# Hybrid mLSTM and pooling step: u, v and the gates begin with two contraction steps of one channel tile

## The chip, the cores and the metric

The kernel runs on one core of one Trainium2 chip. The metric is the device time of one execution, in microseconds (us); several runs of the same program are taken and their median is compared. TensorE multiplies matrices, VectorE and ScalarE work element by element, GpSimd does little here, and SyncE (SP) issues most of the transfers from the chip's main memory.

## What is computed

One step of a flow-matching backbone for 128 prompt tokens and 256 sample tokens, D = 2048 channels, in float32. Everything between the first norm and the output is one layer:

```python
mod = jax.nn.silu(cond) @ ada_w + ada_b          # shift, scale, gate for attention and MLP, 2048 each
h = _rmsnorm(x, norm_w[0]) * (1 + scale_a) + shift_a
proj = h @ w_in
q, k, v, o, g, u = jnp.split(proj, [M, 2 * M, 3 * M, 4 * M, 4 * M + N_GATES * N_HEADS], axis=-1)
...
mix = jnp.concatenate([hm, hp], axis=-1) @ w_out
x = x + gate_a * _rmsnorm(mix, norm_w[1])
h = _rmsnorm(x, norm_w[2]) * (1 + scale_f) + shift_f
y = jnp.square(jax.nn.relu(h @ w1)) @ w2
x = x + gate_f * _rmsnorm(y, norm_w[3])
```

hm comes from a bidirectional mLSTM over q, k, v and the gates g, hp from pooling u. The prompt and the sample have their own conditioning vectors, so every channel has two shifts and two scales.

## The kernel before, in words

**Precision.** Every large product is made of three: each operand is split into a high part (a copy to a narrower form, on ScalarE) and a low part (the difference, on VectorE), and hi·hi, hi·lo and lo·hi are added in PSUM (lines 379 to 381). `load_w` (line 114) loads a weight tile into one of three `raw` buffers from SP's queue (line 120) and splits it (lines 126 and 127).

**The adaLN product** `ada_mat` (line 203) multiplies the two conditioning vectors, as narrow stationary windows of 32 columns, with tiles of `ada_w`. Line 207 sets the tile: for `nk` channel tiles it is 128 partitions by 8/nk contraction rows by 128·nk channels, always 512 KB. A step of two channel tiles needs eight such tiles for shift and scale together, each with four products (eight instructions, line 218). They come from SP's queue (line 214) into four buffers with the tag "ada"; in the very first step half of them use the four buffers "lo". After the last tile ScalarE copies the sums (line 223), TensorE turns them into columns (line 226) and VectorE adds the bias and the norm's weight (lines 234 and 239). The function is a generator: each `next` emits one tile, the last two the copy and the columns. With nk = 2 that is nine `next`, with nk = 1, by line 207, five: four tiles of eight products each.

**x.** Three tiles of 128 tokens are loaded, their squares summed, and `transpose_x` (line 304) turns one channel tile with three TensorE transposes (line 307) and a copy out of PSUM, on ScalarE for odd tiles (line 310) and on VectorE for even ones (line 312). The string `X_ORDER` (line 32) says in which order transposes ("t"), adaLN steps ("a") and the broadcast of the norm factors ("b", lines 196 and 321) are issued. Up to `order.close()` (line 364), TensorE, VectorE and ScalarE run in exactly this order; behind it, and on SP's queue throughout, the builder's scheduler orders the instructions, by the order of the code and by when it takes them to be ready.

**h, u, v and gates.** `ksteps` (line 276) lists eight steps of two channel tiles. `make_h` (line 332) makes h of one step: hm (line 338) on VectorE, hh (line 343) on ScalarE, hl (line 344) on VectorE. In the first call the low part of u's first weights is computed between (line 341). The loop of line 367 runs over the steps, and in each over five chunks: two of u (512 columns each), then v with 384, 384 and 256 columns, the last with the 32 gate columns. A chunk loads its weights, multiplies them into three PSUM banks (one per token tile), and adds the banks into u and v in SBUF: copies on ScalarE in the first step (line 392), adds on VectorE in the others (line 394), gates in line 396. Behind the first three chunks stand three adaLN steps each for the next step's channels (`ADA_STEPS`, line 31), behind the fourth `make_h` of the next step (line 385). Eight PSUM banks serve everything.

The rest (q, k and attention with pooling and gates beside them, o, the output projection, the MLP) follows from line 398 on and isn't touched.

Of the kernel before, what the change touches and what calls it, by code (L numbers as in the profile page):

```python
# [15 lines left out]
KT = D // P  # L16
# [13 lines left out]
N_ADA = 4  # L30
ADA_STEPS = (3, 3, 3, 0, 0)
X_ORDER = "tatatatabtatatatat"
N_VEC = 4
# [5 lines left out]
def hymba_kernel(  # L39
# [20 lines left out]

    # ---------------------------------------------------------------- constants and small inputs
    cst = const.tile([P, N_CST, P], F32, name="cst")
# [32 lines left out]

    # silu(c); for every contraction tile in a row of zeros, so that a window of 32 columns puts it in any pair of rows
    cT = const.tile([P, 16, 38], F32, name="cT")
# [7 lines left out]

    # per-channel parameters as columns: prmT [128, 80 | 96]
    prmT = const.tile([P, 176], F32, name="prmT")
# [4 lines left out]

    # ---------------------------------------------------------------- helpers
    def load_w(pieces, name, n=1024, after=(), later=None):
        """pieces: (column offset in the tile view, dram AP [128, a, b]); returns the hi and lo parts."""
        raw = wp.tile([P, 1024], F32, tag="raw", name=f"raw_{name}", bufs=3)
# [25 lines left out]
    class Feed:  # L142
        """Side work, emitted in steps between the tiles of a large product."""

# [13 lines left out]
    def gemm_T(w, cols, xs, n, evac, feeds=(), korder=(0, 1, 2, 3), name="g", hold=None):  # L158
        """Transposed products: for every 256-column group, out[128 channels, n] in two tiles; groups share the k loop."""
        wv = wview(w)  # L160
# [24 lines left out]
    def rstd_cols(out, ss, n, scale):  # L185
        """out = (ss * scale + eps) ** -0.5, [128, n]"""
        nc.vector.tensor_scalar(out, ss, scale, EPS, op0=ALU.mult, op1=ALU.add)
        nc.gpsimd.tensor_tensor(out, out, mhalf[:, 0:n], op=ALU.pow)

    def bcast_row(col, name, ps=None):  # L190
        """PSUM tile with [p, 128 i + t] = col[t, i] for every partition p."""
        dg = slot(f"dg_{name}")
        dgv = dg[:, 0:NTOK].rearrange("p (i t) -> p i t", t=P)
        nc.vector.tensor_tensor(dgv, ident.unsqueeze(1).to_broadcast([P, 3, P]), col.unsqueeze(2).to_broadcast([P, 3, P]), op=ALU.mult)
        ps = bank(f"bc_{name}") if ps is None else ps
        nc.tensor.matmul(ps[:, 0:NTOK], ones, dg[:, 0:NTOK], start=True, stop=True)
        return ps

    # ---------------------------------------------------------------- adaLN
    mod = const.tile([P, 6, KT, 2], F32, name="mod")  # L200
    aw = ada_w.rearrange("(p j) n -> p j n", j=16)

    def ada_mat(parts, tags=("ada",)):
        """parts: up to four (i, first channel tile), nk channel tiles each, on the tensor engine.
        Row 32 g + 2 b + (0: ctx, 1: latent) of ps holds part b's sum over the contraction tiles j = g (mod 4)."""
        n, nk = len(parts), parts[0][2]
# [24 lines left out]
    def ada_finish(i, k0, nk, ps):  # L231
        """ps [128, nk, 2]: matrix product columns -> mod[i], with what the channel's norm weight adds to it"""
        v = mod[:, i, k0:k0 + nk, :]
# [10 lines left out]
    def ada_vec(i, q):  # L244
        """512 channels, on the vector engine; the tensor engine adds up the partitions"""
        acc = wp.tile([P, 2, 512], F32, tag="adaacc", name=f"ada_acc_{i}_{q}", bufs=1)
# [27 lines left out]

    # ---------------------------------------------------------------- x: statistics and transposes
    ksteps = [(k, 2) for k in range(0, KT, 2)]
    NS = len(ksteps)

    def first_ada():
# [42 lines left out]

    # ---------------------------------------------------------------- h, and u, v, gates (token-major), k outermost
    h = []
# [39 lines left out]
    order.close()  # L364
    for k in range(len(xT), KT):
        transpose_x(k)
    for s in range(NS):
        for ci, (kind, c0, w) in enumerate(chunks):
# [6 lines left out]
            for k in range(nk):  # L375
                xh, xl = h[k0 + k]
                for i in range(3):
# [3 lines left out]
                    nc.tensor.matmul(acc[i][:, 0:n], xl[:, sl], hi[:, k, :], start=False, stop=k == nk - 1)  # L381
            for _ in range(ADA_STEPS[ci]):
                next(ada0, None)
# [15 lines left out]

    # ---------------------------------------------------------------- pooling mixer  # L400
    mix = [None] * KT
# [22 lines left out]

    # ---------------------------------------------------------------- gate rows, stabilisers
    tokc = ((0, 1, 2), (0, 2, 1))
# [76 lines left out]

    # ---------------------------------------------------------------- q, k and attention
    q_sb, k_sb = [None] * NH, [None] * NH
# [15 lines left out]
    def attention(hp):  # L521
        """Two heads."""
        h0 = 2 * hp
# [44 lines left out]
        def update(i, d, wk):  # L568
            """state after the chunk at token tile i in direction d"""
            out = att.tile([P, 2, 129], F32, tag="C", name=f"C1_{hp}_{i}_{d}", bufs=5)  # L570
# [109 lines left out]

    # ---------------------------------------------------------------- o
    mixs = [None] * KT
# [25 lines left out]

    # ---------------------------------------------------------------- output projection
    for k in range(8):  # L710
# [33 lines left out]
    def token_rstd_rows(accs, name, between=None):  # L744
        """PSUM tile with (mean over channels + eps) ** -0.5 of every token, on all partitions"""
        ps = bank(f"tr_{name}")
# [14 lines left out]

    # ---------------------------------------------------------------- gate_f * norm_w[3] as rows
    mlp = ctx.enter_context(tc.tile_pool(name="mlp", bufs=2))
# [12 lines left out]

    # ---------------------------------------------------------------- residual and the MLP's input
    xr = []
# [56 lines left out]

    # ---------------------------------------------------------------- MLP
    hid = {}
# [98 lines left out]
    def done(i, a, b, side=iter(())):  # L936
        """square sum and gate of finished columns, a step of other work in between"""
        jk = mlp.tile([P, 512], F32, tag="jk", name=f"jky{i}_{a}", bufs=1)
        n = a // 512 + (a % 512 > 0)
        nc.scalar.activation(jk[:, 0:b - a], y[i][:, a:b], AF.Square, accum_out=ssy[:, i, n:n + 1])  # L940
        next(side, None)
        nc.vector.tensor_tensor(y[i][:, a:b], y[i][:, a:b], gf[min(i, 1), a // 1024][:, a % 1024:a % 1024 + b - a], op=ALU.mult)
# [6 lines left out]
    def residual(i):  # L949
        """norm and residual of a token tile, in pieces"""  # L950
        dst = y_prompt[0] if i == 0 else y_sample[0, (i - 1) * P:i * P]
# [5 lines left out]
    def last_part(ws):  # L957
        """the last 512 columns, token tile by token tile; the last tile in halves"""
        side = iter(())
# [88 lines left out]
```

## Time and profile before

| | |
|---|---|
| runs | 1767.98 us median of 3 (1766.83 to 1768.8) |
| profiled execution, first to last instruction | 1766.4 us, its own whole time isn't given apart from this span |
| mean granted TensorE clock | 0.994 |
| moved from main memory | 313.98 MB read, 184 GB/s over the span |
| start of the first step's u products | 30.71 us |
| steps of the loop of line 367 begin at | 30.71, 55.73, 78.53, 104.11 us ... |

The profile lists each instruction by its line, engine and operand names, "out<-in". PE is TensorE's matmul unit, DVE VectorE, ACT ScalarE, SPq the sync engine's queue. A row of the time view gives the start, the duration, the instruction and, in brackets, the idle time ahead of it and what ended it; instructions of one kind are merged ("x20"). A row of the view by stretches gives the length, then busy time and count of PE, weight loads, DVE, ACT and POOL, the granted clock, the busy share of the DMA engines and GB/s; asked for one line, only the engines that run it appear. In the view of waits a row names who waited for whom, the sum, the number of times and the longest. In the chain of waits that ended last, a row gives start, length and what the chain went through. Matmul durations include their latency: products that follow each other overlap, and their spacing is less than the duration.

### The profile page before, as it was taken

How to read it: one execution, taken by the hardware profiler on the slowest of the kernel's cores; microseconds unless marked ns; L12 is line 12 of the kernel's file. 1: busy time of each engine (PE TensorE's matmuls, PEld its weight loads, DVE VectorE, ACT ScalarE, POOL GpSimd, SP SyncE). 2: the span in 40 equal slices, each digit the busy share in tenths (PEclk: the TensorE clock that was granted, in tenths of full speed). 3: DMA queues.
4: the chain of work that ended last, by engine and by line, in shares of the span. 5: the costliest groups of instructions: out<-in, count | busy, mean ns of one | idle time of the engine just before them, and what ended most of it. 6: DMA issues, size and time to landing. Idle time of an engine off the chain costs nothing.

```text
span 1766.4 us, 24738 instructions
## 1 busy us (share of the span) xinstructions
PE 1719.2 (97%) x9643; PEld 1539.2 (87%) x9643; DVE 1067.4 (60%) x1756; ACT 627.3 (36%) x1047; POOL 129.7 (7%) x172
## 2 busy tenths in 40 slices
PE   6999999998999999999999999999999999999997
PEld 3777898887999989988988988988988998998986
DVE  3667877787898849763546644475444443443446
ACT  4322343443434336532432432332332332332332
POOL 0000021222101133110000000000000000000100
PEclk9999999999999999999999999999999999999999
DMA  9888988887777774574345544454434354344543
GB/s 304 279 263 286 299 261 231 253 251 213 232 238 235 237 250 156 185 225 131 120 130 162 175 130 121 130 167 122 129 120 131 120 168 131 120 130 136 165 141 107
DMA packets 250436, 326.15 MB, mean 185 GB/s; under 512 B 14096, under 2 KB 185808, under 8 KB 249936
## 3 DMA queue, kind: packets, MB, share of 16 engines
q1 hardware_dynamic: 242096, 303.74, 54.1%
q0 software_dynamic: 6560, 18.97, 4.3%
q10 hardware_dynamic: 1664, 1.87, 0.3%
q8 instruction: 75, 1.23, 0.3%
q14 instruction: 41, 0.34, 0.1%
HBM read 313.98 MB, written 10.55 MB: 184 GB/s over the span
## 4 chain that ended last, share of the span: by engine, by line
PE 86%; DMA 5%; issue 3%; DVE 2%; POOL 2%; ACT 1%; SPq 0%; ACTq 0%; DVEq 0%; POOLq 0%
PE y L855 10%; PE y L856 10%; PE y L857 10%; PE acc_w L135 9%; PE acc_w L137 9%; PE acc_w L136 9%; DMA ada_raw<-in_ada_w_dram 3%; PE acc_wo L135 3%; PE acc_wo L136 2%; PE acc_wo L137 2%; PE ada L218 2%; PE acc_o L135 1%; PE acc_o L137 1%; PE acc_o L136 1%; PE u L379 1%
## 5 line engine op out<-in xcount | busy, mean ns | idle before, releaser
L127 DVE TENSOR_TENSOR lo_w<-raw_w,hi_w 128x1024 fp32r<-128x1024 f32 x256 | 313.9, 1226 | 440.7 <-ACT hi_w L126 440.3
L126 ACT ACTIVATE hi_w<-raw_w 128x1024 fp32r<-128x1024 f32 x256 | 271.3, 1060 | 666.2 <-PE acc_w L136 302.1
L135 PE MATMUL acc_w<-h2h,hi_w 128*128 128x386 f32 x1024 | 347.8, 341 | 2.4 <-ACT h2h L805 2.4
L137 PE MATMUL acc_w<-h2h,lo_w 128*128 128x386 f32 x1024 | 347.5, 339 | 0.0
L136 PE MATMUL acc_w<-h2l,hi_w 128*128 128x386 f32 x1024 | 347.2, 339 | 0.0
L257 DVE SCALAR_TENSOR_TENSOR ada_acc<-ada_raw,sg,ada_acc 128x512 f32<-128x512 f32 x330 | 237.5, 767 | 21.8 <-DMA ada_raw<-in_ada_w_dram 21.7
L135 PEld LDWEIGHTS acc_w<-h2h,hi_w 128*128 128x128 f32 x1024 | 193.9, 190 | 5.2 <-ACT h2h L805 3.0
L136 PEld LDWEIGHTS acc_w<-h2l,hi_w 128*128 128x128 f32 x1024 | 193.8, 189 | 0.9 <-issue 0.4
L137 PEld LDWEIGHTS acc_w<-h2h,lo_w 128*128 128x128 f32 x1024 | 193.5, 189 | 0.0
L218 PE MATMUL ada<-ada_raw,cT 128*32 128x256 f32 x832 | 61.5, 397 | 5.1 <-DMA ada_raw<-in_ada_w_dram 5.0
L879 DVE TENSOR_TENSOR y<-y,y 128x512 f32<-128x512 f32 x81 | 55.7, 691 | 11.8 <-PE y L857 11.3
L126 ACT ACTIVATE hi_wo<-raw_wo 128x1024 fp32r<-128x1024 f32 x32 | 34.1, 1067 | 67.1 <-PE acc_wo L136 27.9
L846 ACT ACTIVATE z<-z,bz 128x128 f32<-128x128 f32 (+1 forms) x128 | 47.9, 442 | 11.3 <-DVE z L844 11.2
L127 DVE TENSOR_TENSOR lo_wo<-raw_wo,hi_wo 128x1024 fp32r<-128x1024 f32 x32 | 38.7, 1218 | 19.3 <-ACT hi_wo L126 19.3
L379 PE MATMUL v<-hi_v,hh 128*128 128x384 f32 (+1 forms) x144 | 49.0, 341 | 0.0
L381 PE MATMUL v<-hi_v,hl 128*128 128x384 f32 (+1 forms) x144 | 47.2, 328 | 0.0
L380 PE MATMUL v<-lo_v,hh 128*128 128x384 f32 (+1 forms) x144 | 46.9, 326 | 0.0
L774 POOL DMA_DIRECT2D gf_dram<-gfT x1 | 0.5, 519 | 626.8 <-DVE bz L843 626.8
L135 PE MATMUL acc_k<-hh,hi_k 128*128 128x384 f32 x128 | 45.4, 355 | 0.0
L218 PEld LDWEIGHTS ada<-ada_raw,cT 128*32 128x32 f32 x832 | 19.8, 110 | 28.9 <-issue 14.5
L135 PE MATMUL acc_o<-hh,hi_o 128*128 128x384 f32 x128 | 44.7, 349 | 0.0
L135 PE MATMUL acc_q<-hh,hi_q 128*128 128x384 f32 x128 | 44.4, 347 | 0.0
(940 smaller groups left out, 3621.1 us busy)
## 6 DMA issues: line engine op xcount, KB each, us to landing
raw_w<-in_w_dram SPq DMA_DIRECT2D x256, 512.0 KB, 3.7
ada_raw<-in_ada_w_dram SPq DMA_DIRECT2D x192, 512.0 KB, 5.1
raw_wo<-in_w_out_dram SPq DMA_DIRECT2D x32, 512.0 KB, 4.9
raw_u<-in_w_in_dram SPq DMA_DIRECT2D x16, 512.0 KB, 7.4
raw_q<-in_w_in_dram SPq DMA_DIRECT2D x16, 512.0 KB, 5.8
raw_k<-in_w_in_dram SPq DMA_DIRECT2D x16, 512.0 KB, 5.2
raw_o<-in_w_in_dram SPq DMA_DIRECT2D x16, 512.0 KB, 5.3
raw_v<-in_w_in_dram SPq DMA_DIRECT2D x16, 384.0 KB, 7.8
```

The costliest lines, as they stand in the source:

```text
L126: nc.scalar.activation(hi[:, 0:n], raw[:, 0:n], AF.Copy)
L127: low = lambda: nc.vector.tensor_tensor(lo[:, 0:n], raw[:, 0:n], hi[:, 0:n].bitcast(F32), op=ALU.subtract)
L135: nc.tensor.matmul(ps, lh, rh, start=start, stop=False)
L136: nc.tensor.matmul(ps, lh, rl, start=False, stop=False)
L137: mm3.ins = nc.tensor.matmul(ps, ll, rh, start=False, stop=stop).ins
L218: nc.tensor.matmul(ps[32 * g:32 * g + 32, 0:w], cT[:, j, 6 - 2 * b:38 - 2 * b], raw[:, a, :], start=b == 0 and j < 4, stop=b == n - 1 and ...
L257: nc.vector.scalar_tensor_tensor(acc[:, g, :], raw[:, a, :], cj, acc[:, g, :], op0=ALU.mult, op1=ALU.add)
L379: nc.tensor.matmul(acc[i][:, 0:n], xh[:, sl], hi[:, k, :], start=k == 0, stop=False)
L855: nc.tensor.matmul(acc, xh[:, s], hi, start=k == 8 * ch, stop=False)
L856: nc.tensor.matmul(acc, xh[:, s], lo, start=False, stop=False)
L857: nc.tensor.matmul(acc, xl[:, s], hi, start=False, stop=k == 8 * ch + 7)
L879: nc.vector.tensor_tensor(dst, acc[i], dst, op=ALU.add)
```

## The change

The first two channel tiles become steps of their own, so there are nine steps instead of eight: channel tiles 0, 1, then 2 and 3, and so on. X_ORDER holds four adaLN steps (instead of eight) and eleven transposes (instead of nine), of which seven stand behind the broadcast. The remaining five transposes (of seven before, which stood between `make_h(0)` and the loop) are written inside the first step: three behind the first u chunk's products, two behind the second's. The number of adaLN steps behind each chunk now depends on the size of the step that they prepare: 2, 2 and 1 for one channel tile, 3, 3 and 3 for two. By line 218's indices the products for a single channel tile are 128 columns wide instead of 256, and rows of the adaLN load are 512 B instead of 1 KB; weight tiles of u and v hold half as much. Comments and docstrings were dropped; they aren't shown.

```diff
-ADA_STEPS = (3, 3, 3, 0, 0)
-X_ORDER = "tatatatabtatatatat"
+X_ORDER = "tatatatabttttttt"
...
-    ksteps = [(k, 2) for k in range(0, KT, 2)]
+    ksteps = [(0, 1), (1, 1)] + [(k, 2) for k in range(2, KT, 2)]
     NS = len(ksteps)
+    ada_steps = {1: (2, 2, 1, 0, 0), 2: (3, 3, 3, 0, 0)}
...
     order.close()
-    for k in range(len(xT), KT):
-        transpose_x(k)
     for s in range(NS):
...
-            for _ in range(ADA_STEPS[ci]):
+            if s == 0 and ci < 2:
+                for _ in range(3):
+                    if len(xT) < KT:
+                        transpose_x(len(xT))
+            for _ in range(ada_steps[ksteps[s + 1][1]][ci] if s < NS - 1 else 0):
                 next(ada0, None)
```

## Prediction

> **What bounds the kernel now.** I read the page first, then the stretch in which u, v and the gates are computed, step by step, then its instructions in order of time, then the waits of the sync queue.
>
> ```profile
> span 1766.4 us, 24738 instructions
> PE 1719.2 (97%) x9643; PEld 1539.2 (87%) x9643; DVE 1067.4 (60%) x1756; ACT 627.3 (36%) x1047; POOL 129.7 (7%) x172
> ```
>
> The span is 1766.4 us; the page gives no other time for this execution. The runs' median, 1767.98, lies 1.6 us above the span, which I take as what lies around it: a change of the span goes to the median unchanged. TensorE is busy for 97%, so nothing after the first stages can give much; what the change can reach is the start, and the order of the steps behind it. These are rows of busy time for the stretch 10 to 30 us and for the first four steps of the loop of line 367, all engines:
>
> ```profile
> 10.00:20.00 10.00, 5.03 (x26) 2.09 (x26) 1.19 (x5) 7.29 (x13) 0.88 (x1) 1.00 1.05 369
> 20.00:30.00 10.00, 9.94 (x88) 5.43 (x87) 4.27 (x12) 3.24 (x6) 0.00 (x0) 1.00 1.09 354
> 30.71:55.73 25.02, 22.70 (x161) 17.39 (x160) 12.16 (x25) 14.87 (x30) 0.00 (x0) 1.00 0.91 302
> 55.73:78.53 22.80, 22.37 (x161) 17.22 (x159) 15.21 (x31) 7.00 (x12) 0.00 (x0) 1.00 0.88 282
> ```
>
> From 10 to 30 us the DMA engines are full (share above 1). From 55.73 on TensorE is busy for 22.37 of 22.80 us: the loop is TensorE's. The first step takes 25.02, so TensorE stands for 2.3 us there. The instructions at the start, in order of time:
>
> ```profile
> 16.53 1.08 PE L218 MATMUL ada<-ada_raw,cT 128*32 128x256 f32 x8 [1.13 <-DMA ada_raw<-in_ada_w_dram]
> ...
> 18.37 1.08 PE L218 MATMUL ada<-ada_raw,cT 128*32 128x256 f32 x8
> ...
> 21.95 0.64 PE L218 MATMUL ada<-ada_raw,cT 128*32 128x256 f32 x8
> ...
> 22.52 0.91 PE L196 MATMUL bc_rx<-dg_rx,cst 128*128 128x384 f32 x2
> ...
> 23.27 0.49 PE L307 MATMUL xt<-cst,xtok 128*128 128x128 f32 x3
> ...
> 26.97 0.64 PE L218 MATMUL ada<-ada_raw,cT 128*32 128x256 f32 x8
> ...
> 27.54 0.66 PE L307 MATMUL xt<-cst,xtok 128*128 128x128 f32 x4
> ...
> 28.11 0.61 PE L226 MATMUL ada<-cst,ada_sb 128*128 128x4 f32 x4
> ...
> 28.57 2.38 PE L307 MATMUL xt<-cst,xtok 128*128 128x128 f32 x20
> ...
> 29.28 1.41 DVE L338 SCALAR_TENSOR_TENSOR hm<-xT,mod,rbc 128x128 f32<-128x128 f32 x4
> 29.67 1.60 ACT L343 ACTIVATE hh<-hm,mod 128x128 fp32r<-128x128 f32 x4 [0.30 <-DVE hm L338]
> ...
> 31.27 1.22 DVE L127 TENSOR_TENSOR lo_u<-raw_u,hi_u 128x1024 fp32r<-128x1024 f32 x1
> ...
> 32.54 0.50 PE L380 MATMUL u<-lo_u,hh 128*128 128x512 f32 x1 [1.35 <-DVE lo_u L127]
> ```
>
> The eighth adaLN tile is read at 26.97; line 226 turns the sums into columns at 28.11; hm, hh and lo_u follow; from 32.54 u's products run without a stop. Until then the 20 transposes (2.38 us, 0.119 each) fill TensorE's time. The row "x4" at 27.54 holds one transpose more than the nine tiles of X_ORDER give: one that the code puts behind make_h(0) runs ahead of line 226. So where TensorE would stand, the builder pulls later work forward.
>
> **Part by part.** *The start of u.* The first step needs four adaLN tiles instead of eight. Tiles are 512 KB still, so the fourth is read where the fourth is read now, at 21.95, ending 0.64 later, about 22.6. The broadcast of line 196 takes until 23.27 now, 0.75. Seven transposed tiles now stand between it and line 226 in the hand-made order: 21 x 0.119 = 2.5, so line 226 starts at about 25.8 (now 28.11). From there to hm are 1.17 us now (29.28 less 28.11). One channel tile has half the pieces: hm 2 x 0.35 = 0.70, then lo_u of half the width, 0.61, and hl. 25.8 + 1.17 + 0.70 + 0.61 = 28.3, with 0.1 for hl: the products run from **28.4** instead of 32.54, 4.1 earlier. The first u weights (256 KB) stand behind four tiles on the sync queue instead of eight, so they are no later than now.
>
> *The five transposes.* 15 x 0.119 = 1.8 us on TensorE, three copies on ScalarE, two on VectorE, no DMA. Between line 226's end (26.1) and 28.3 TensorE has 2.2 us without other work, and the "x4" row shows that such work is pulled forward. I cost them at 0; if they really run behind u's products, 1.8.
>
> *The second tile's adaLN.* It used to be over before u began; now it runs inside the first short step. Here are line 218's own instructions in one step, and from the gate rows of a later stage the nearest 128-column products with narrow weights:
>
> ```profile
> 55.73:78.53 22.80, 4.28 (x64) 1.66 (x64) 1.00 0.88 282
> ...
> 221.64 0.27 PE L457 MATMUL ps_a<-cst,lf 128*8 128x128 f32 x1
> 221.65 0.28 PE L456 MATMUL ps_a<-cst,gsb 128*8 128x128 f32 x1
> 221.75 0.27 PE L457 MATMUL ps_a<-cst,lf 128*8 128x128 f32 x1
> ```
>
> 64 instructions of 256 columns take 4.28 us. The second tile has 64 of 128 columns: 2.14 if the time goes by columns, 4.28 if by instructions. The gate rows start 0.01 apart in two column groups and 0.11 apart in one, so issue isn't the limit: I take 2.14 and keep 4.28 for the range. Its four loads move on SP from ahead of the first u load to behind it, where two of them wait for buffers that the first tile leaves free by about 19.4, long before 28.4; GpSimd's queue carries none of them.
>
> *Products.* A step of 22.80 less 4.28, less 0.55 for line 226 and 0.43 of waiting (rows below) leaves 17.5 for two channel tiles, 8.77 for one. First short step 8.77 + 2.14 + 0.3 = 11.2; second 8.77 + 4.28 + 0.55 = 13.6.
>
> *A new wait.* The second short step prepares two channel tiles, eight adaLN tiles through four buffers, with half the products to hide them:
>
> ```profile
> 43.19 5.65 DMA ada_raw<-in_ada_w_dram
> 66.51 5.65 DMA ada_raw<-in_ada_w_dram
> 89.32 6.51 DMA ada_raw<-in_ada_w_dram
> ...
> 48.89 0.64 PE L218 MATMUL ada<-ada_raw,cT 128*32 128x256 f32 x8 [0.96 <-DMA ada_raw<-in_ada_w_dram]
> ...
> 51.75 1.60 ACT L343 ACTIVATE hh<-hm,mod 128x128 fp32r<-128x128 f32 x4 [0.29 <-DVE hm L338]
> ...
> 72.20 0.64 PE L218 MATMUL ada<-ada_raw,cT 128*32 128x256 f32 x8 [0.43 <-DMA ada_raw<-in_ada_w_dram]
> 73.40 0.55 PE L226 MATMUL ada<-cst,ada_sb 128*128 128x4 f32 x4
> ```
>
> The eighth tile takes the fourth's buffer and lands 5.65 after its request. From its read to hh of the next channel tile are 51.75 - 48.89 + 0.80 = 3.66. So 9.3 us lie between the fourth tile's read and the next u. TensorE's work in between: four more tiles 2.1, line 226 0.55, and v's three chunks. With full chunks (half of 17.5, about 8.5) that is over 11, and nothing is lost; with half chunks (4.3) it is 6.9. **Stall: 2.4 us** in front of the third step. Behind it wait all products of that step; VectorE's adds catch up meanwhile.
>
> *Sum.* Products from 28.4, plus 11.2, 13.6 and 2.4: the step of channels 2 and 3 starts at 55.6 instead of 55.73. **-0.1 us**, since the loop behind it is unchanged. 1767.98 - 0.1 = **1767.9**.
>
> *Work beside it.* The added step brings 15 more adds into u and v on VectorE and copies in half the time on ScalarE. ScalarE's groups of the first step:
>
> ```profile
> L392 ACT ACTIVATE u<-u 128x512 f32<-128x512 f32 x6 | 3.5, 596 | 4.1 <-PE u L381 3.9
> L392 ACT ACTIVATE v<-v 128x384 f32<-128x384 f32 x6 | 2.7, 485 | 3.2 <-PE v L381 3.1
> L126 ACT ACTIVATE hi_u<-raw_u 128x1024 fp32r<-128x1024 f32 x2 | 2.1, 1054 | 0.3 <-DMA raw_u<-in_w_in_dram 0.3
> L126 ACT ACTIVATE hi_v<-raw_v 128x768 fp32r<-128x768 f32 x2 | 1.7, 846 | 0.4 <-DMA raw_v<-in_w_in_dram 0.4
> ...
> 48.40 0.50 SPq L120 DMA_DIRECT2D raw_u<-in_w_in_dram  x1
> ```
>
> ScalarE's 14.87 busy us in the first step hold 3.8 of these splits; halving them leaves at most 13.0 for a short step in which TensorE has 11.2. I cost this at 0, since the kernel's eight PSUM banks let the copies of one chunk lag behind the next, and keep 1.8 for the range. Five more weight loads take SP 0.5 us each; it mostly waits (below).
>
> TensorE's clock is the other unknown. After the longest wait in these steps the granted clock fell:
>
> ```profile
> 95.88 0.64 PE L218 MATMUL ada<-ada_raw,cT 128*32 128x256 f32 x8 [1.82 <-DMA ada_raw<-in_ada_w_dram]
> ...
> 96.00:100.00 4.00, 4.00 (x21) 3.49 (x18) 2.03 (x9) 1.34 (x4) 0.00 (x0) 0.61 1.04 349
> ```
>
> A wait of 1.82 us was followed by four microseconds at 0.61, a loss of 4 x 0.39 = 1.6. The Trainium skill, "TensorE: Matmul & The Clock Gate", Part 1 (the HAM clock gate), says the clock halves only after an idle window of about 3.4 us; by that rule the stall of 2.4 costs no clock and the sum stays 1767.9. The trace doesn't agree: 1.82 sufficed once, while 0.96 and 0.43 did not.
>
> **The rivals.** *Slower: the sync queue.* SP issues in order, and a weight load that waits for one of three raw buffers holds the adaLN tiles behind it.
>
> ```profile
> SPq L120 <- DVE lo_u L127: 32.3, 10, 5.5
> 50.68 8.30 SPq L120 DMA_DIRECT2D raw_v<-in_w_in_dram  x3
> ```
>
> Loads waited 32.3 us in ten times, 3.2 each. If one such wait falls in front of the second short step's last tiles, the stall is 5.6 and the clock falls: 3.2 + 1.6 - 0.1 = +4.7, **1772.7**. It decides from 3.6 us of delay in all. For it: the queue alternates these loads now. Against: half-size splits free the raw buffers sooner.
>
> *Clock alone:* the 2.4 us stall costs 1.6 more: **1769.5**.
>
> *Narrow rows.* For one channel tile an adaLN row is 512 B instead of 1 KB, and no row here shows such loads. If the time went by rows, a tile would take 2.8 instead of 1.4 us (18.37 less 16.53 bounds it at 1.8 now): the fourth lands near 26.5, four later than now, the second tile's after 38; some +2.5, **1770.5**. The Trainium skill, "DMA: Bandwidth & Descriptors", Specifications, gives 512 B as the least transfer at line rate; by it this rival costs nothing. No run here shows it.
>
> *Faster.* The builder pulls products or tiles so that the stall vanishes (-2.5), and the shifted queue also loses the wait of 1.82 with its slow clock (-3.4): -5.9, **1762.1**. For it: waits of 0.43 to 1.82 differ from step to step though the code is the same. Against: nothing in the change aims there.
>
> *Not as described:* the transposes go ahead of u's products after all. That is already in my sum.
>
> **Numbers.** About 0.2%, 3.5 us, is what a measurement of this kernel can tell from no change. Forecast 0.45; clock 0.12; narrow rows 0.06; slower by the queue 0.20; faster 0.17, of which 0.02 stays within 3.5. Faster 0.15, same 0.65, slower 0.20. Range 1763.5 to 1772.5: it takes in the uncovered transposes (+1.8), adaLN by instructions (+2.1), ScalarE (+1.8) and most of the two outer rivals.
>
> **What would show it.** Line 226's first two products near 25.8, u without a stop from 28.4, the third step's u near 55.6 after an idle of about 2.4 with hh or the adaLN tile as its releaser; line 218's 64 narrow products at about 2.1 us; no transposes behind u. I am wrong if u starts later than 30, if the short steps together take over 29 us or under 25, or if the difference arises behind 56 us.

## The result and the profile after

The changed kernel took 1783.09 us (median of 4 runs, 1780.3 to 1786.92), the kernel before 1767.42 (4 runs, 1766.83 to 1768.8): a ratio of 1.0084, 95% interval 1.0065 to 1.0103, 15 to 16 us slower where no change was forecast. The profiled execution of the changed kernel took 1785.05 us.

In the changed kernel weights are loaded in L119 and split in L125 (ScalarE) and L126 (VectorE), adaLN tiles are loaded in L213, read in L217 and turned into columns in L225; L307 is the transposes, L343 hh, L377 to L379 the products of u and v, L394 the copies of the first step, L396 the gates. The page's head, and then the busy time of all engines in stretches (PE, weight loads, VectorE, ScalarE, GpSimd; then granted clock, share of the DMA engines, GB/s):

```profile
span 1783.3 us, 24925 instructions
PE 1728.6 (97%) x9707; PEld 1546.8 (87%) x9707; DVE 1075.1 (60%) x1782; ACT 627.0 (35%) x1053; POOL 128.8 (7%) x172
```

```profile
10.00:20.00 10.00, 4.59 (x40) 2.58 (x41) 1.19 (x5) 7.20 (x13) 0.88 (x1) 1.00 1.10 333
20.00:30.00 10.00, 8.28 (x68) 6.15 (x69) 6.58 (x16) 4.19 (x9) 0.00 (x0) 0.92 1.11 298
28.00:32.00 4.00, 3.99 (x11) 2.89 (x11) 1.54 (x4) 0.74 (x2) 0.00 (x0) 0.57 0.75 199
44.00:48.00 4.00, 2.40 (x5) 1.01 (x5) 2.33 (x6) 2.48 (x7) 0.00 (x0) 0.67 0.15 36
48.00:52.00 4.00, 4.00 (x19) 2.34 (x22) 2.24 (x4) 0.97 (x2) 0.00 (x0) 0.50 0.64 186
27.77:65.89 38.12, 33.76 (x239) 23.36 (x240) 20.32 (x49) 14.69 (x35) 0.00 (x0) 0.87 0.71 220
65.89:89.40 23.51, 23.51 (x158) 18.66 (x159) 15.29 (x32) 7.30 (x13) 0.00 (x0) 0.93 0.87 276
```

The two short steps together (27.77 to 65.89) take 38.1 us, where the one step before took 25.0; the DMA engines are used for 0.71 of it and TensorE's clock is 0.87. The step of channels 2 and 3, at 55.73 before, begins at 65.89. TensorE's own instructions there, in order of time:

```profile
22.19 0.64 PE L217 MATMUL ada<-ada_raw,cT 128*32 128x128 f32 x16
...
25.81 0.28 PE L225 MATMUL ada<-cst,ada_sb 128*128 128x4 f32 x2
27.77 1.28 PE L377 MATMUL u<-hi_u,hh 128*128 128x512 f32 x2 [1.68 <-ACT hh L343]
...
31.80 1.15 PE L307 MATMUL xt<-cst,xtok 128*128 128x128 f32 x9
32.87 1.08 PE L217 MATMUL ada<-ada_raw,cT 128*32 128x128 f32 x32
...
36.10 0.49 PE L307 MATMUL xt<-cst,xtok 128*128 128x128 f32 x3
...
37.29 0.55 PE L307 MATMUL xt<-cst,xtok 128*128 128x128 f32 x3
...
45.60 1.65 PE L377 MATMUL u<-hi_u,hh 128*128 128x512 f32 x3 [2.44 <-ACT hi_u L125]
...
65.89 0.79 PE L377 MATMUL u<-hi_u,hh 128*128 128x512 f32 x1 [1.41 <-ACT hh L343]
```

Up to 27.77 the landmarks are as forecast. The five transposes (9 + 3 + 3 instructions) then run behind u's products, and the second short step's u waits for hi_u, a split on ScalarE. What ScalarE did before that, and the sync queue:

```profile
37.66 1.57 ACT L394 ACTIVATE u<-u 128x512 f32<-128x512 f32 x3 [3.30 <-PE xt L307]
...
39.63 1.62 ACT L394 ACTIVATE u<-u 128x512 f32<-128x512 f32 x3
41.07 1.34 ACT L394 ACTIVATE v<-v 128x384 f32<-128x384 f32 x3
42.18 0.89 ACT L343 ACTIVATE hh<-hm,mod 128x128 fp32r<-128x128 f32 x2
42.87 2.16 ACT L394 ACTIVATE v<-v 128x384 f32<-128x384 f32 x6
44.78 1.29 ACT L125 ACTIVATE hi_u<-raw_u 128x512 fp32r<-128x512 f32 x2
```

```profile
38.93 8.78 SPq L119 DMA_DIRECT2D raw_v<-in_w_in_dram  x4
...
52.16 9.94 SPq L213 DMA_DIRECT2D ada_raw<-in_ada_w_dram  x7
```

What the sync queue waited for from 38 to 66 us (sum, times, longest):

```profile
SPq L213 <- PE ada L217: 10.3, 7, 3.9
SPq L119 <- DVE lo_u L126: 7.0, 2, 6.8
```

The first row of ScalarE is the finding: a copy of u, whose products were done at about 32, starts at 37.66, and what ends its wait is a transpose. Line 327 of the kernel gives u_sb the tags of the x tiles ("x0" to "x2", one buffer each): u is written where x stood, and not before the last transpose has read x. ScalarE works through its list in order here, so everything behind that copy stands too; it then works without a pause past 45.6, and the hi_u that TensorE waits for stands behind all the copies. The sync queue stands twice: 6.8 us until lo_u has been made from a raw buffer and the buffer is free, then 3.9 us until TensorE has read the first of four adaLN tiles. So four of the eight adaLN tiles for channels 2 and 3 are asked for between 33 and 39 us, and the other four only from 52 on (the row "x7" has them first, then three of the next step).

### The profile page after: what moved, and what is told of

Same layout as the page of the kernel before. It is cut to its first block, busy times and chain, and to the rows that moved or that the text cites. A ratio compares the mean times of both kernels' runs of the same rounds, so it can differ in the third digit from the quotient of the medians.

```text
span 1783.3 us, 24925 instructions
## 1 busy us (share of the span) xinstructions
PE 1728.6 (97%) x9707; PEld 1546.8 (87%) x9707; DVE 1075.1 (60%) x1782; ACT 627.0 (35%) x1053; POOL 128.8 (7%) x172
## 4 chain that ended last, share of the span: by engine, by line
PE 85%; DMA 6%; issue 4%; DVE 2%; POOL 2%; ACT 1%; SPq 0%; DVEq 0%; POOLq 0%; ACTq 0%
PE y L857 10%; PE y L859 10%; PE y L858 10%; PE acc_w L134 10%; PE acc_w L135 10%; PE acc_w L136 10%; DMA ada_raw<-in_ada_w_dram 3%; PE acc_wo L134 2%; PE acc_wo L135 2%; PE acc_wo L136 2%; PE ada L217 2%; PE u L377 1%; PE acc_o L134 1%; PE u L378 1%; PE u L379 1%
## 5 line engine op out<-in xcount | busy, mean ns | idle before, releaser
L126 DVE TENSOR_TENSOR lo_w<-raw_w,hi_w 128x1024 fp32r<-128x1024 f32 x256 | 313.7, 1225 | 442.3 <-ACT hi_w L125 441.9
L125 ACT ACTIVATE hi_w<-raw_w 128x1024 fp32r<-128x1024 f32 x256 | 271.3, 1060 | 670.2 <-PE acc_w L135 303.7
L217 PE MATMUL ada<-ada_raw,cT 128*32 128x256 f32 (+1 forms) x896 | 63.8, 385 | 3.7 <-DMA ada_raw<-in_ada_w_dram 3.6
L881 DVE TENSOR_TENSOR y<-y,y 128x512 f32<-128x512 f32 x81 | 55.7, 691 | 11.7 <-PE y L859 11.3
L125 ACT ACTIVATE hi_wo<-raw_wo 128x1024 fp32r<-128x1024 f32 x32 | 34.1, 1067 | 67.9 <-DMA raw_wo<-in_w_out_dram 26.9
L126 DVE TENSOR_TENSOR lo_wo<-raw_wo,hi_wo 128x1024 fp32r<-128x1024 f32 x32 | 38.7, 1216 | 19.1 <-ACT hi_wo L125 19.1
L377 PE MATMUL v<-hi_v,hh 128*128 128x384 f32 (+1 forms) x144 | 48.6, 337 | 0.0
L217 PEld LDWEIGHTS ada<-ada_raw,cT 128*32 128x32 f32 x896 | 22.4, 112 | 29.0 <-issue 16.3
L379 PE MATMUL v<-hi_v,hl 128*128 128x384 f32 (+1 forms) x144 | 46.6, 324 | 0.0
L377 PE MATMUL u<-hi_u,hh 128*128 128x512 f32 x96 | 40.0, 427 | 5.5 <-ACT hh L343 3.1
```

Of the source, the lines that this page charges most:

```text
L125: nc.scalar.activation(hi[:, 0:n], raw[:, 0:n], AF.Copy)
L126: low = lambda: nc.vector.tensor_tensor(lo[:, 0:n], raw[:, 0:n], hi[:, 0:n].bitcast(F32), op=ALU.subtract)
L217: nc.tensor.matmul(ps[32 * g:32 * g + 32, 0:w], cT[:, j, 6 - 2 * b:38 - 2 * b], raw[:, a, :], start=b == 0 and j < 4, stop=b == n - 1 and ...
L377: nc.tensor.matmul(acc[i][:, 0:n], xh[:, sl], hi[:, k, :], start=k == 0, stop=False)
```

## The experiments

Theory 1: the transposes, now behind u's products, hold u's copies through the shared buffer. The rest has two candidates from the prediction, the narrow rows and the second short step with eight adaLN tiles. All ratios are to the kernel before on the same chip, with 95% intervals; 0.1% is 1.8 us. Line numbers shift by a few from kernel to kernel; the names tell what a row is.

**Transposes ahead of u again.**

```diff
     order.close()
+    for k in range(len(xT), KT):
+        transpose_x(k)
...
-            if s == 0 and ci < 2:
...
-                        transpose_x(len(xT))
```

> The change, with its five late transposes back between make_h(0) and the loop; the two short steps stay. Theory 1 (u's copies into SBUF use the buffers of x's token tiles, so they wait for the last transpose; ScalarE stands behind them and everything that ScalarE does next is late): with the transposes done before u begins the copies wait for nothing, u of the second short step begins near 40.5 us instead of 45.6, u of the third step at 56 to 58 instead of 65.9, the time is 1767 to 1771. Theory 2 (the short steps themselves: eight adaLN tiles through four buffers, and weight loads that hold SP's queue): the third step begins after 64 as in the change, the time is above 1778.

Measured: 1.0049 (1.0034 to 1.0064). The landmarks came (second u at 39.9, third step at 55.44; the prediction's sum had 55.6), the time didn't: it lies between the two theories, and that third step takes 27.9 us instead of 22.8. Two stretches, one from the first short step into the second and one from there into the third, then ScalarE:

```profile
28.00:44.00 16.00, 15.99 (x150) 12.20 (x149) 10.16 (x25) 12.45 (x29) 0.00 (x0) 1.00 0.78 242
44.00:64.00 20.00, 17.80 (x123) 10.68 (x122) 13.90 (x33) 5.27 (x10) 0.00 (x0) 1.00 1.04 337
```

```profile
59.91 1.06 ACT L125 ACTIVATE hi_u<-raw_u 128x1024 fp32r<-128x1024 f32 x1 [3.43 <-DMA raw_u<-in_w_in_dram]
66.27 0.85 ACT L125 ACTIVATE hi_v<-raw_v 128x768 fp32r<-128x768 f32 x1 [5.30 <-DMA raw_v<-in_w_in_dram]
```

The DMA engines are at 0.78 from 28 to 44 us and full afterwards, and weights arrive late. So part of the loss, 0.35 of 0.84%, goes with the place of the transposes, and the rest sits in the transfers or what hangs on them. Of the 5 us by which this step is longer, some 1.7 are TensorE's clock, 0.94 over the step; another kernel below has 27.3 us for it at a clock of 1.00.

**u in a place of its own.** The transposes stay behind u; u lies in the first 1024 channels of the x tiles, whose transposes are long done.

```diff
-    u_sb = [pre.tile([P, M], F32, tag=f"x{i}", name=f"u{i}") for i in range(3)]
+    u_sb = [t[:, 0:M] for t in x_tok]
```

> The change, but u lies in the first half of x's token tiles as a part of the same tile, so that its copies wait only for the transposes of the first eight channel tiles and not for the five late ones; no memory is added. Theory 1: ScalarE no longer stands from 34.4 to 37.7, the splits of the second short step come before 43, u of that step begins near 42 and of the third near 59 to 61 (the 1.8 us of transposes and the slow clock at 28 us remain), the time is 1771 to 1776. Theory 2: no difference to the change, above 1779.

Measured: 1.0042 (1.0025 to 1.0060), second u at 41.6, third step at 58.1. ScalarE's copies of u:

```profile
29.39 1.75 ACT L394 ACTIVATE xtok<-u 128x512 f32<-128x512 f32 x3 [0.24 <-PE u L379]
...
34.04 1.56 ACT L394 ACTIVATE xtok<-u 128x512 f32<-128x512 f32 x3
```

They run as soon as the products are done, 37.66 has become 29.39. Taking away the wait by either way gives back about the same, and this edit leaves the transposes where they are, so the shared buffer is a cause. How much it costs is less sure: the interval here, 1.0025 to 1.0060, lies below that of the changed kernel's first measurement, but overlaps that of its second further down (1.0043 to 1.0097).

**The transposes behind u, but full steps**, and the same with u in its own place.

```diff
-    for k in range(len(xT), KT):
-        transpose_x(k)
...
+            if s == 0 and ci < 2:
+                for _ in range(4):
+                    if len(xT) < KT:
+                        transpose_x(len(xT))
```

> The kernel before with its steps of two channel tiles, and only its last seven transposes moved behind u's first two chunks (four and three). Theory 1: ScalarE waits with u's copies until the last transpose near 42 us, six PSUM banks are held and v begins late; 3 to 7 us are lost, 1771 to 1775. Theory 2: within 1.5 us of the kernel before plus at most 1 us for the uncovered transposes, 1767 to 1769.

> The kernel before with its last seven transposes behind u's two first chunks, and u kept in the upper channels' place of the x tiles, so that u's copies wait only for transposes that were made long before. Shared buffer theory: ScalarE's waits for the last transpose (3.9 and 2.2 us in the kernel without the second edit) are gone, and no cost or gain is left: -2 to +2. Rival: transposes behind u cost TensorE's time at this place whoever waits: +1 to +4.

Measured: 1.0012 (0.9997 to 1.0027) and 1.0006 (0.9987 to 1.0025). ScalarE of the first:

```profile
42.83 0.49 ACT L310 ACTIVATE xT<-xt 128x384 f32<-128x384 f32 x1 [3.92 <-PE xt L307]
...
45.55 1.58 ACT L394 ACTIVATE u<-u 128x512 f32<-128x512 f32 x3 [2.23 <-PE xt L307]
```

The same wait is there, 2.23 us, and costs nothing that can be measured: the second step begins at 56.2 instead of 55.7. The 3 to 7 us that theory 1 expected here didn't come. So the wait alone isn't enough; it costs time together with the short steps. That full chunks leave TensorE enough other work to hide it fits this, but wasn't tested by itself.

**Narrow rows alone**, in the kernel before: its first adaLN step made one channel tile at a time, which takes one `next` more.

```diff
-X_ORDER = "tatatatabtatatatat"
+X_ORDER = "tatatatabtataatatat"
...
-        for k0, nk in ksteps:
-            yield from ada_mat([(0, k0, nk), (1, k0, nk)], ("ada", "lo") if k0 == 0 else ("ada",))
+        for k0, nk in [(0, 1), (1, 1)] + ksteps[1:]:
+            yield from ada_mat([(0, k0, nk), (1, k0, nk)], ("ada", "lo") if k0 < 2 else ("ada",))
```

> The kernel before, its steps of two channel tiles, with one difference: the adaLN products of channel tiles 0 and 1 are made one tile at a time, from eight tiles with rows of 512 B instead of eight with rows of 1 KB, all ahead of u. Theory 1 (narrow rows): eight tiles of 512 KB at 305 instead of 355 GB/s take 1.9 us more, u begins at about 32.5 and all behind it comes later by that, +2 to +8. Theory 2 (second short step): at most the 1.9 us of a later start, +0 to +2, and no step behind it longer than before (25.0, 22.8, 25.6 us).

Measured: 1.0025 (1.0006 to 1.0045), u's products from 32.8. From 14 to 30 us, this kernel and the kernel before:

```profile
14.00:30.00 16.00, 10.91 (x155) 6.84 (x156) 3.69 (x11) 5.37 (x11) 0.88 (x1) 1.00 1.15 301
```

```profile
14.00:30.00 16.00, 13.88 (x109) 7.05 (x110) 5.06 (x15) 6.80 (x13) 0.88 (x1) 1.00 1.09 352
```

The stretch with rows of 512 B moves 301 GB/s, the one with rows of 1 KB 352, with the engines full in both, and u begins 2.1 us later, as worked out. Some weights with longer rows are in both; from 18 to 22 us it is 290 against 348.

**Short steps without narrow rows**: all transposes ahead of u, and both first tiles' adaLN made together ahead of u, with X_ORDER as before.

```diff
-        for k0, nk in ksteps:
+        for k0, nk in [(k, 2) for k in range(0, KT, 2)]:
...
+            for _ in range((3, 3, 3, 0, 0)[ci] if 0 < s < NS - 1 else 0):
```

> The changed kernel's two short steps of u, v and the gates, all transposes ahead of u's first products, but the adaLN products of channel tiles 0 and 1 as before: one step of eight tiles with rows of 1 KB, all ahead of u. Before = 0, the changed kernel about +15 us, the same with only the transposes moved back about +8. Theory 1, the rest of the loss comes from rows of 512 B (305 instead of 355 GB/s, so the transfers fall behind): the rest is gone, 0 to +2, u's products from about 30.5 and the third step (channels 2, 3) at about 54 to 55 and 23 us long. Theory 2, it comes from the second short step, in which eight adaLN tiles go through four buffers and the sync queue carries the third step's first weights behind them: the rest stays, +5 to +8, with the third step longer than 25 us or the second short step longer than 16.

Measured: 1.0041 (1.0026 to 1.0056), third step 27.3 us long (56.74 to 84.04). The narrow rows aren't needed for the loss, so theory 1 of this expectation falls for the bulk of it.

**The eight adaLN tiles spread over both short steps**, transposes ahead.

```diff
+            for _ in range(((3, 2, 2, 2, 0), (2, 2, 1, 0, 0))[s][ci] if s < 2 else (3, 3, 3, 0, 0)[ci] if s < NS - 1 else 0):
```

> As the changed kernel with the transposes moved back ahead of u, but the eight adaLN tiles that prepare channels 2 and 3 are spread over both short steps: behind the first step's chunks stand 3, 2, 2 and 2 adaLN steps (the second tile's five and four for channels 2 and 3), behind the second's 2, 2 and 1. Rows of 512 B for channel tiles 0 and 1 stay. Theory 2: the third step's first weights no longer stand behind eight tiles, it takes about 23 instead of 27.9 us and begins near 55, and the time falls from about +8 to +1 to +3. Theory 1: the transfers are as late as before, the third step still takes over 26 us, +6 to +8.

Measured: 1.0023 (1.0012 to 1.0035): about half of what was left, between the two theories. The two short steps, and the step behind them:

```profile
27.77:56.73 28.96, 25.98 (x219) 17.94 (x218) 17.25 (x44) 16.30 (x37) 0.00 (x0) 1.00 0.91 281
56.73:80.98 24.25, 24.12 (x164) 18.23 (x165) 17.80 (x37) 6.37 (x10) 0.00 (x0) 1.00 0.93 299
```

By its first u product the third step begins at 56.73 and not near 55, after a wait of 2.04 us for hi_u, and is 24.25 us long (about 23 was expected); the last v products of the second short step still run in it, until 59.7. In the same set the changed kernel ran once more:

> The changed kernel once more, on the chip of these runs: about +15 us (1.0084 was measured, 1.0065 to 1.0103). Its profile should have the same landmarks: u's first product near 27.8, the second short step's near 45.6, the third step's near 65.9.

Measured: 1.0070 (1.0043 to 1.0097), landmarks 27.8, 44.1 and 63.0, the last two 1.5 and 2.9 us earlier than in the first profile. The granted clock makes about this difference: from 28 to 32 it is 1.00 (0.57 in the first profile, 1.7 us lost), from 44 to 52 it is 0.63 and 0.94 (0.67 and 0.50).

**Four adaLN tiles less for channels 2 and 3**, in the kernel with the transposes ahead, in the changed kernel, in the changed kernel with u in its own place, and, as a control, in the kernel before. TensorE does the same work; the scale of channels 2 and 3 is made from the shift's tiles, so it is left out of the result.

```diff
+                if (i, k0) == (1, 2):
+                    raw = kept[j0]
+                else:
+                    raw = kept[j0] = wp.tile(...)
+                    nc.sync.dma_start(raw, ...)
```

> As the changed kernel with all transposes ahead of u's products, but the adaLN step for channels 2 and 3 loads four tiles instead of eight: the second four products sets read the first four tiles again, so TensorE does the same work on 2.1 MB less (scale of channels 2 and 3 is not computed from its own weights). Theory 3, the two short steps ask for more bytes than the transfers can bring: eight tiles and half of the weights are 5.3 MB, at 355 GB/s 14.8 us, in a step in which TensorE has work for 13.6. Then 2.1 MB less is 5.9 us less of transfer: the third step, 27.9 us in that kernel, takes 22 to 23.5, and of its +8 us at most +2 to +3 are left. Rival: the smaller pieces themselves (ScalarE, VectorE, waits with a slow clock) cost the time: the third step stays over 26 and +6 to +8 stay.

> The changed kernel itself, with the same four adaLN tiles less for channels 2 and 3 (their scale is not computed from its own weights). If the two causes, ScalarE's copies behind the transposes and the bytes, stand beside each other, the time falls from +15 to about +8 to +10, with the second short step's u still beginning late, near 45. If the wait of ScalarE delays the transfers as well and is the whole cause here (the sync queue stands still during it), little changes at its start but the third step begins at about 60 instead of 63 to 66: +8 to +11. If bytes alone were the cause: +2 to +3.

> The changed kernel with both suspected causes taken away: four adaLN tiles less for channels 2 and 3 (their scale is not computed from its own weights), and u kept in the upper channels' place of the x tiles, so that its copies do not wait for the transposes behind u's products. The transposes stay behind u. If the two causes are the whole loss: -2 to +2 against before, with the second short step's u near 41 and the third step's at 54 to 56. If the transposes behind u cost time of their own, by the slow clock after the wait of 1.7 us ahead of u and by TensorE's 1.8 us: +3 to +5, with the third step near 58.

> The control for the runs with four adaLN tiles less: the kernel before with the same four tiles left out (the scale of channels 2 and 3 is not computed from its own weights). If the lateness of the transfers belongs to the short steps, before loses none of its time to these tiles and gains little: its first step, 25.0 us, can lose at most the 2.3 us in which TensorE stands, 0 to -2.5. If 2.1 MB less is worth the same anywhere near the start, it gains 5 us or more, and the runs with fewer tiles say nothing about the change.

Measured:

| | eight tiles | four tiles |
|---|---|---|
| kernel before | 0.9998 (unchanged, run again) | 1.0011 (0.9997 to 1.0025) |
| changed | 1.0084, 1.0070 | 1.0025 (1.0009 to 1.0042) |
| changed, transposes ahead | 1.0049 | 0.9999 (0.9984 to 1.0013) |
| changed, u in its own place | 1.0042 | 1.0003 (0.9987 to 1.0019) |

The kernel before gains nothing by fewer tiles, the short steps gain 0.4 to 0.6%. With the wait and four tiles gone, nothing is left of the loss that can be measured, and the two add up: 0.25% left by fewer tiles alone and 0.42 to 0.49% left without the wait make 0.67 to 0.74%, of 0.70 to 0.84%. The expectation for the changed kernel with four tiles less missed: 8 to 11 us were to be left by either account with the wait, and some 4.4 (1.6 to 7.4) are. These runs don't show that there is no third cause, for transfer time that is saved here also makes up for what narrow rows cost. The two short steps together and the step behind them, in the kernel with the transposes ahead and four tiles less:

```profile
27.80:54.30 26.50, 25.64 (x226) 19.10 (x225) 18.58 (x44) 16.32 (x36) 0.00 (x0) 1.00 0.83 258
54.30:77.00 22.70, 22.70 (x158) 17.12 (x159) 17.24 (x39) 7.47 (x13) 0.00 (x0) 1.00 0.93 303
```

**Is it enough to ask earlier?** Short steps without narrow rows, the adaLN tiles for channels 2 and 3 asked for from the first short step on; then, beside it, weights loaded for two chunks at a time, also in the spread version.

```diff
-            for _ in range((3, 3, 3, 0, 0)[ci] if 0 < s < NS - 1 else 0):
+            for _ in range(((2, 2, 1, 1, 1), (1, 1, 0, 0, 0))[s][ci] if s < 2 else ...
...
+        if s < 2 and ci < 4 and (s, ci // 2) != (0, 0):
+            ... pair[0] = load_w([(0, wv_in[:, ks, b:b + 2 * n])], ..., 2 * n, after, later)
```

> As the kernel with short steps of u, v and the gates and the first two tiles' adaLN made together ahead of u, but the eight adaLN tiles for channels 2 and 3 are asked for from the first short step on, as before: behind its chunks stand 2, 2, 1, 1 and 1 adaLN steps, behind the second's 1 and 1. So the same bytes as before at about the same places, and only the steps of u, v and the gates are short. If the late asking (no adaLN tile in the first short step, eight in the second) is what the transfers lack, the +0.41% of that kernel falls to 0 to +0.15% and the third step takes 22 to 24 us instead of 27.3. If half-size weight tiles in three buffers are enough to make the transfers late, +0.25% or more stays and the step stays over 25.

> As the kernel with short steps whose adaLN tiles are asked for early (+0.48%), but in the two short steps the weights of two neighbouring chunks are loaded and split together, as one tile of 512 or 384 KB (u's two chunks, v's first two; the first step's u stays as it is). Products, copies and adds stay in the same pieces. If half-size weight tiles in three buffers are what makes the transfers late, the loss falls to 0 to +0.2%, and the waits for weights between 46 and 60 us (3.1, 2.2 and 1.9 us) are gone or under 1. If the pieces of products, copies and adds are the cause, or the total of bytes, +0.35% or more stays.

> The same pairing of weight loads in the kernel with both adaLN products of one channel tile and the eight tiles for channels 2 and 3 spread over both short steps (+0.23%, u's products from 27.8). If half-size weight tiles are the cause, this is the version in which an early start of u could be kept: -0.1 to +0.1%, third step near 56. If not: +0.2 to +0.3% as without the pairing.

Measured: 1.0048 (1.0030 to 1.0065), 1.0046 (1.0029 to 1.0064), 1.0031 (1.0014 to 1.0047). None of the three brings the hoped-for gain: neither late asking alone nor half-size weight tiles are what is left there. VectorE and TensorE of the first of them show what is:

```profile
56.87 1.58 DVE L344 SCALAR_TENSOR_TENSOR hl<-hm,mod,hh 128x128 fp32r<-128x128 f32 x4 [0.17 <-ACT hh L343]
58.37 1.02 DVE L394 TENSOR_TENSOR v<-v,v 128x384 f32<-128x384 f32 x2
59.30 0.45 DVE L126 TENSOR_TENSOR lo_v<-raw_v,hi_v 128x288 fp32r<-128x288 f32 x1
59.66 1.22 DVE L126 TENSOR_TENSOR lo_u<-raw_u,hi_u 128x1024 fp32r<-128x1024 f32 x1
```

```profile
58.97 1.05 PE L217 MATMUL ada<-ada_raw,cT 128*32 128x256 f32 x10 [0.95 <-DVE v L394]
```

TensorE waits for an addition on VectorE, which works almost without a pause; the splits lo_v and lo_u stand behind its additions.

**The second short step's additions left out**, with the transposes ahead, and with the adaLN tiles asked for early. Channel tile 1 is then missing from u, v and the gates (15 additions and 3 for the gates).

```diff
-            for i in range(3):
+            for i in range(3) if s != 1 else ():
```

> As the changed kernel with all transposes ahead of u's products (+0.49%), but the second short step's products are not added into u, v and the gates (15 additions of VectorE and 3 for the gates left out, so channel 1 is missing from u, v and the gates). These additions are the only work that nine steps have and eight don't. If VectorE is what the third step waits for (there, lo_u of its first weights stood at 58.41 behind additions, hm and hl, and u's second product waited until 59.68), the third step falls from 27.9 to under 24.5 us and the loss to 0 to +0.2%. If the transfers alone are late, its second u tile still waits for raw_u near 59 to 60 and +0.35% or more stays.

> The same 18 additions left out (channel 1 is missing from u, v and the gates) in the kernel with short steps whose adaLN tiles are made together and asked for as early as before (+0.48%). VectorE theory: 0 to +0.2%, and the waits between 54 and 61 us go. Transfers: the waits of 3.1, 2.2 and 1.9 us for weights stay, and +0.35% or more.

Measured: 1.0047 (1.0029 to 1.0065) and 1.0007 (0.9994 to 1.0019). The two differ sharply. With the tiles asked for late the additions cost nothing that can be measured, and hi_u still waits for its weights (ScalarE, first kernel); with the tiles asked for early nearly all of the loss goes with them (VectorE, second kernel: lo_u at 55.60 instead of 59.66):

```profile
60.09 1.06 ACT L125 ACTIVATE hi_u<-raw_u 128x1024 fp32r<-128x1024 f32 x1 [3.32 <-DMA raw_u<-in_w_in_dram]
```

```profile
55.60 1.22 DVE L126 TENSOR_TENSOR lo_u<-raw_u,hi_u 128x1024 fp32r<-128x1024 f32 x1 [0.21 <-ACT hi_u L125]
```

How an addition makes a weight late can be followed in the two kernels that ask early, whose sync queues run alike, to 0.1 us, up to 46.9. First with the additions, then without:

```profile
47.27 1.89 DVE L394 TENSOR_TENSOR u<-u,u 128x512 f32<-128x512 f32 x3 [0.82 <-PE u L381]
49.07 0.68 DVE L126 TENSOR_TENSOR lo_u<-raw_u,hi_u 128x512 fp32r<-128x512 f32 x1
49.78 0.80 SPq L119 DMA_DIRECT2D raw_v<-in_w_in_dram  x2
```

```profile
45.77 1.29 DVE L126 TENSOR_TENSOR lo_u<-raw_u,hi_u 128x512 fp32r<-128x512 f32 x2 [0.33 <-ACT hi_u L125]
47.40 0.92 SPq L119 DMA_DIRECT2D raw_v<-in_w_in_dram  x2
```

The second lo_u stands behind u's additions, its raw buffer comes free at 49.75 instead of 47.06, and the next weights are asked for 2.4 us later. So the additions act through the transfers. They are no limit by themselves: with four tiles less they are all still there, and nothing of the loss is left (0.9999).

**The kernel before once more.**

> The kernel before, unchanged, for a second profile of it and for how far two runs of one program differ here: ratio 1.000 within 0.002. Its profile shows whether the delays that all changed kernels gather behind 280 us against the first profile of before (3 to 5 us, with the same instructions in the same order) belong to the changes or to the execution that was profiled: if to the execution, this profile gathers 2 to 5 us there too.

Measured: 0.9998 (0.9978 to 1.0018). Its q begins at 206.1 us, 4.2 earlier than in the first profile, and by 665 us it is 1.8 later, with the same instructions in the same order. Most of the 4.2 us is one step, that of channels 4 and 5: 25.6 us in the first profile (78.53 to 104.11), 22.4 in the second (77.42 to 99.78), where neither the wait of 1.82 us nor the slow clock behind it occurs. Around the adaLN columns near 282 us, the second profile and the first:

```profile
276.00:290.00 14.00, 11.02 (x61) 10.45 (x62) 12.22 (x23) 4.93 (x8) 0.00 (x0) 0.88 0.78 244
```

```profile
280.00:294.00 14.00, 11.43 (x76) 10.85 (x77) 12.66 (x23) 5.89 (x10) 0.00 (x0) 1.00 0.84 271
```

So delays of the size that the changed kernels gather behind 280 us, 3 to 5 us, come with the execution and need no change; landmarks of single profiles are good to some 4 us, the ratios decide.

No kernel tried here is faster than the kernel before.

## Why the prediction was wrong

*The start of u: right.* Line 225 at 25.81 (25.8 forecast), u's first product at 27.77 (28.4).

*The five transposes: the step that failed first.* They were costed at 0 because "the "x4" row shows that such work is pulled forward". They weren't: TensorE stood for 1.68 us ahead of u, and they ran behind it. The other end, 1.8 us, was wrong too, because it priced their TensorE time. The price lies with those who wait for them: ScalarE's copies, through a buffer that the prediction didn't look up, and all that ScalarE had queued. It is 0.35 to 0.42% (6 to 7 us) by the first measurement of the changed kernel against the two without the wait, 0.21 to 0.28% (4 to 5 us) by the second, whose interval overlaps theirs.

*The second tile's adaLN: right.* 32 products in 1.08 us make 64 in about 2.1 (2.14).

*Narrow rows: a rival given 0.06 that is partly true.* Alone they cost 0.25% (0.06 to 0.45), 4.4 us. The size forecast for it, 2.5 us, lies inside. The Trainium skill, "DMA: Bandwidth & Descriptors", Specifications, calls 512 B the least transfer at line rate; these runs don't agree: 301 GB/s against 352.

*The short steps, 11.2 and 13.6 us, and the stall of 2.4: wrong in the changed kernel, nearly right without the wait for transposes.* In the changed kernel they took 17.8 (27.77 to 45.60) and 20.3 (45.60 to 65.89), 38.1 together, far over the 29 that the prediction named as a sign of being wrong. With the transposes ahead they took 11.5 and 15.5 (28.41, 39.90, 55.44), against 11.2 and 16.0. The sum's "55.6" for the third step was then met by 55.44, in part by luck, since no stall of 2.4 us stands there. And the sum still failed: *"since the loop behind it is unchanged"* doesn't hold, for the loop takes over late transfers, and its first step became 5 us longer.

*The new wait in front of the third step: right in kind, wrong in place.* The limit was seen (eight tiles through four buffers beside half the products) but priced as one stall of 2.4 us. Four tiles less are worth 0.4 to 0.6% (7 to 10 us). With the transposes ahead most of that falls behind the third step's start, where weights come late: four tiles less bring that start from 55.44 to 54.30, and the next step's from 83.33 to 77.03.

*Slower by the sync queue, given 0.20: the right direction, too small and at another buffer.* It needed 3.6 us of delay and priced 4.7 us. With the transposes ahead the queue's longest wait between 30 and 66 us is 5.3 us, but for TensorE to read an adaLN tile, not for a raw buffer.

*ScalarE and VectorE costed at 0: wrong here, though not everywhere.* That the banks "let the copies of one chunk lag behind the next" overlooks that the next weights' splits stand behind the copies in the same queue; where the copies wait for nothing, the 0 holds (11.5 against 11.2). The additions were called work beside; where the adaLN tiles are asked for early they cost 0.4% (1.0048 against 1.0007), through the raw buffers.

*The clock.* The stall ahead of the second short step was 2.44 us, and 48 to 52 ran at 0.50. The wait of 1.68 ahead of u was followed, in the stretch 28 to 32, by 0.57 in the changed kernel's first profile and by 1.00 in its second; in the one with u in its own place it was also 1.00:

```profile
28.00:32.00 4.00, 3.99 (x41) 3.13 (x44) 2.30 (x5) 3.04 (x6) 0.00 (x0) 1.00 0.72 198
```

So the prediction's "1.82 sufficed once" is a chance, not a threshold, and the second profile of the kernel before does without that wait altogether. The Trainium skill, "TensorE: Matmul & The Clock Gate", Part 1, asks for an idle window of about 3.4 us and calls the window free-running. A wait of half that length, 1.68 us, brought the clock to 0.57 here, so the length doesn't agree; that the same wait does it in one execution and not in another agrees with a window that runs freely, but no run here shows the window.

What stays open: why the wait for transposes costs nothing with full steps, and how the loss divides between narrow rows and the crowded step in the changed kernel itself; their single costs (0.25% and 0.41%) add up to more than the 0.42 to 0.49% in which both are present.

## What to carry to other kernels

Before costing moved work, look up which buffers its readers and writers share: a moved read delays every write into the same place, and an engine that works in order passes that wait on to all that stands behind. A step cut in half halves the work that hides, but neither the transfers for the next step nor the additions per step, so compare each of these with the half step. And when a landmark is met but the time isn't, look for the debt (late transfers) that the next step pays.

## What the runs showed of the hardware

With the DMA engines full in both, the start with adaLN rows of 512 B brought 301 GB/s and the one with rows of 1 KB 352 GB/s (14 to 30 us, tiles of 512 KB; 290 and 348 from 18 to 22 us). The same wait of 1.68 us of TensorE ahead of the same product was followed, from 28 to 32 us, by a granted clock of 0.57 in one execution of the changed kernel and 1.00 in another. Two executions of one program differed by 4.2 us at the start of q and by 1.8 us the other way at 665 us.
